# First modulation vectors: half of the columns by split products, half in full precision; first tiles transposed beside their copies

## The chip, the cores and the metric

The kernel runs on one core of one Trainium2 chip. The metric is the device time of one execution in microseconds (us); the time of a kernel is the median of several runs. The engines are named as in the profile: PE (matrix products), PEld (its weight loads), DVE (VectorE), ACT (ScalarE), POOL (GpSimd) and SP, which here only issues transfers. ACT issues some transfers too. Each engine works through its own instructions in the order in which they stand in the program.

## What is computed

One layer of a generative model: 2048 latent tokens and 256 context tokens of width 1024 pass a gated linear recurrence in both directions, then a gated feed-forward layer with a short convolution. What matters here is the very start. Two conditioning vectors, `c` for latent tokens and `c_ctx` for context tokens, give shift, scale and gate vectors by one product with `w_ada` (1024 by 6144):

```
sc_lat, sc_ctx = jax.nn.silu(c), jax.nn.silu(c_ctx)
m_l = (sc_lat @ w_ada[l] + b_ada[l])[:, None, :]
m_c = sc_ctx @ w_ada[l] + b_ada[l]
sh1, sc1, g1, sh2, sc2, g2 = jnp.split(m_l, 6, axis=-1)
hl = modulate(rmsnorm(lat, norm_g[l, 0]), sh1, sc1)
hc = modulate(rmsnorm(cx, norm_g[l, 0]), csh1, csc1)
yc, yl = hgrn2_mixer(hc, hl, ...)      # begins with h @ w_in, 1024 by 5120
```

Nothing of the recurrence can begin before the first 2048 columns of that product (shift and scale of the mixer) are there for both kinds of tokens. The other columns are worked out later, beside other work.

## The kernel before

All tokens are cut into 18 tiles of 128. Three tiles make a unit of 384 columns; six units follow each other for each of 8 heads. The first unit is context tile 0, context tile 1 and latent tile 0. A tile is normalized in place (ACT squares it and sums, DVE and POOL make the reciprocal root `rs`, DVE multiplies; helper `normalize`, L100 to L105, called by `early_x`), transposed by PE in two groups `g` of four 128-wide blocks (`transpose_mod`, L112), and multiplied and shifted by the modulation vectors A and B while it is copied out of PSUM: by ACT (L116) or by DVE (L119). The result `hm` is then split into a rounded part `hh` (ACT, L80) and a remainder `hl` (DVE, L81) by the helper `split`. All large products are sums of three products of such parts, rounded with rounded, rounded with remainder and remainder with rounded (`mm3`, L356 to L358); weights are split the same way into `wh` and `wl`, `vh` and `vl`, after their load into a tile `raw`.

The first stage (L189 to L232) works out the modulation vectors. `w_ada` comes in 16 transfers of 512 KB, `i` = 0 for the shift and `i` = 1 for the scale, for each of 8 row blocks `k`; `i` = 0 is issued by ACT, `i` = 1 by SP. The tiles `wada` have 13 buffers, which the weights of head 0 use after them. For each, PE makes two products of 512 columns in full fp32 precision with the two activated vectors `silv` as weights; each such product stands in the trace as two MATMUL records. They collect in four PSUM tiles `mps`. ACT copies these to `m2` (L216), PE turns them by 16 small transposes into `mt` (L220), and DVE makes B and A of them (L223 to L225). Then come the two groups of the first three tiles:

```
for g in range(2):
    for j, hm in enumerate(hms):
        transpose_mod(staged[j], hm, g, p0s, A1[m], B1[m], "tr", 3, (g + j) % 2)
        put_split(hm, 0, j, ks)
```

After that stands the normalization of four more tiles (`early_x(3)` to `early_x(6)`), whose transposes and splits are spread among the products of unit 0 of head 0: `unit` gets them as a list `todo`, and `tick`, called after each group of three products, takes the next one when it is due. In that first unit, `ticks = [0, 20]`: the six of them are due at even steps over 20 groups, the first one at once. From head to head the order is a pipeline: `load_feat` and `load_vg` load and split the weights of a head (five transfers of 512 KB for head 0).

A planner in the language's layer orders the instructions on each engine by its own estimate of their times, so the order in the program need not be that of the source. A transfer waits until the transfer eight places before it has landed; SP holds all transfers behind one that waits.

Of the kernel before, what the change touches and what calls it, by code (L numbers as in the profile page):

```python
# [23 lines left out]
KT = 8  # L24
# [24 lines left out]
def body(ctx, tc, a, out):  # L49
    nc = tc.nc  # L50
    pe, act, dve, pool, sp = nc.tensor, nc.scalar, nc.vector, nc.gpsimd, nc.sync
# [27 lines left out]
    def split(h, l, src):  # L79
        act.activation(h, src, AF.Copy)  # L80
        dve.tensor_tensor(l, src, h.bitcast(F32), OP.subtract)  # L81
# [22 lines left out]
        else:  # L104
            dve.tensor_scalar(xt, xt, rs, None, OP.mult)  # L105

    def transpose_mod(xt, hm, g, psp, A, B, tag, bufs, on_act):

        tp = psp.tile([128, 4, 128], F32, name="tp", tag=tag, bufs=bufs)
        for j in range(4):  # L110
            k = g * 4 + j
            pe.transpose(tp[:, j, :], xt[:, k * 128:(k + 1) * 128], ident)  # L112
        for j in range(4):
            k = g * 4 + j
            if on_act:
                act.activation(hm[:, k, :], tp[:, j, :], AF.Identity, bias=B[:, k:k + 1],  # L116
                               scale=A[:, k:k + 1])
            else:
                dve.tensor_scalar(hm[:, k, :], tp[:, j, :], A[:, k:k + 1], B[:, k:k + 1],  # L119
                                  OP.mult, OP.add)  # L120

    ch = ctx.enter_context(ExitStack())
    rawp = pool_(ch, "rawp", 2)
# [62 lines left out]
    with ExitStack() as c0:  # L186
# [2 lines left out]
        act.activation(sil, vec[:, V_C:V_C + 16], AF.Sigmoid)  # L189
        dve.tensor_tensor(sil, sil, vec[:, V_C:V_C + 16], OP.mult)  # L190
        silv = sil.rearrange("p (two k) -> p k two", two=2)
        mps = [p0s.tile([2, 512], F32, name=f"mps{n}") for n in range(4)]
# [10 lines left out]
        for k in range(KT):  # L203
            for i in range(2):
                wt = p0.tile([128, D], F32, name="wada", tag="wada", bufs=13)
                (sp if i else act).dma_start(
                    wt, a["w_ada"][k * 128:(k + 1) * 128, i * D:(i + 1) * D])
                for n in range(2):
                    pe.matmul(mps[2 * i + n], silv[:, k, :], wt[:, n * 512:(n + 1) * 512],
                              start=k == 0, stop=k == KT - 1)  # L210
            if 3 <= k < 6:
                early_x(k - 3)
        head0 = load_feat(0, p=p0, tag="wada", bufs=13)
        m2 = [rawp.tile([2, 2, 512], F32, name="m2", tag="raw") for _ in range(2)]
        for n in range(4):
            ada_done = act.activation(m2[n // 2][:, n % 2], mps[n], AF.Copy)  # L216
        m2f = [m.rearrange("p a b -> p (a b)") for m in m2]
        mt = p0s.tile([128, 16, 2], F32, name="mt")
        for j in range(16):
            pe.transpose(mt[:, j, :], m2f[j // 8][:, j % 8 * 128:(j % 8 + 1) * 128],  # L220
                         ident[0:2, 0:2])
        for i in (1, 0):
            dve.tensor_tensor(B1[i], mt[:, 0:8, i], vec[:, V_BA:V_BA + 8], OP.add)  # L223
            dve.tensor_tensor(A1[i], mt[:, 8:16, i], vec[:, V_BA + 8:V_BA + 16], OP.add)
# [54 lines left out]
    def mixer_scan():  # L279
# [82 lines left out]
        def unit(h, w, u, tiles, todo, fine=False):  # L362
# [1066 lines left out]
```

## Time and profile before

| | us |
|---|---|
| median of 3 runs | 2864.17 (2862.56 to 2865.4) |
| the profiled execution's own time | 2865.12 |
| its span, from first to last instruction | 2863.1 |
| PE busy in it | 2805.9 (98%) |
| DVE busy | 2110.5 (74%) |
| ACT busy | 1174.4 (41%) |
| first product of unit 0 starts | 41.52 |
| first product of unit 1 starts | 70.78 |

How to read it: PE is busy nearly all the time once the first unit has begun, so what the first 75 us lose or gain is found at the end again unless something later absorbs it. All places in time below are counted in us from the start of the span. A row of the timeline gives start, duration, engine, line, operation, output and inputs, how many instructions are merged in the row, and in brackets how long the engine had sat idle and for what. Durations of products overlap, so their rate is read from the distance of their starts.

### The profile page before, as it was taken

The page shows a single profiled execution, that of the slowest core. Times are in us where ns is not written, and L with a number is a line of the kernel's source. Part 1 is how long each engine was busy: PE and PEld are TensorE (multiplying, and loading weights), DVE is VectorE, ACT ScalarE, POOL GpSimd, SP SyncE. Part 2 cuts the span into 40 slices and gives each one's busy share as a digit, 9 for nine tenths or more (in the row PEclk, how much of TensorE's full clock was granted, in tenths as well). Part 3 has the DMA queues.
Part 4 walks back from the last instruction along what each step waited for, and adds up shares of the span by engine and source line. Part 5 has one row for each costly group of instructions (what it writes and reads, how often), then busy time and mean ns, then how long its engine had stood idle before and what let it go on. Part 6 is the DMA issues. An engine that isn't in the chain of part 4 may idle for free.

```text
span 2863.1 us, 43709 instructions
## 1 busy us (share of the span) xinstructions
PE 2805.9 (98%) x16016; PEld 2506.1 (88%) x16016; DVE 2110.5 (74%) x3690; ACT 1174.4 (41%) x2515; POOL 594.3 (21%) x1028
## 2 busy tenths in 40 slices
PE   7999999999999999998999799999999999999999
PEld 4999999999999999997888688888888888887887
DVE  5766666677666666577987698887888887677887
ACT  5433333365333333333555444444444444333343
POOL 2111111121111111111111353343444432000001
PEclk9999999999999999999999899999999999999999
DMA  6222222222222222135677622225522224887663
GB/s 236 69 80 77 84 79 78 78 86 81 85 90 71 84 69 87 62 94 183 266 290 276 257 88 89 82 81 176 206 88 71 77 89 136 284 298 251 196 203 122
DMA packets 202911, 386.56 MB, mean 135 GB/s; under 512 B 26692, under 2 KB 117828, under 8 KB 197448
## 3 DMA queue, kind: packets, MB, share of 16 engines
q1 hardware_dynamic: 199960, 375.51, 39.1%
q10 hardware_dynamic: 2736, 8.26, 0.8%
q8 instruction: 126, 2.06, 0.3%
q14 instruction: 89, 0.73, 0.1%
HBM read 281.70 MB, written 101.99 MB: 134 GB/s over the span
## 4 chain that ended last, share of the span: by engine, by line
PE 89%; DVE 4%; DMA 3%; ACT 2%; issue 1%; POOL 1%; SPq 0%; DVEq 0%; ACTq 0%; POOLq 0%
PE z L358 10%; PE z L356 10%; PE z L357 10%; PE y L1263 4%; PE y L1262 4%; PE y L1261 4%; PE zc L741 3%; PE zd L741 3%; PE zd L738 3%; PE zc L738 3%; PE zc L740 3%; PE zd L740 3%; PE za L741 3%; PE za L738 3%; PE za L740 3%; PE kv L574 2%
## 5 line engine op out<-in xcount | busy, mean ns | idle before, releaser
L356 PE MATMUL z<-vh,hh 128*128 128x256 f32 (+1 forms) x1024 | 300.3, 293 | 0.0
L358 PE MATMUL z<-vh,hl 128*128 128x256 f32 (+1 forms) x1024 | 293.5, 287 | 0.0
L357 PE MATMUL z<-vl,hh 128*128 128x256 f32 (+1 forms) x1024 | 293.3, 286 | 0.0
L356 PE MATMUL z<-hh,wh 128*128 128x384 f32 x768 | 264.0, 344 | 0.7 <-ACT hh L80 0.7
L357 PE MATMUL z<-hl,wh 128*128 128x384 f32 x768 | 258.5, 337 | 0.5 <-DVE hl L81 0.5
L358 PE MATMUL z<-hh,wl 128*128 128x384 f32 x768 | 258.7, 337 | 0.0
L1263 PE MATMUL y<-wd,ml 128*128 128x512 f32 x600 | 234.0, 390 | 2.3 <-DVE ml L81 2.1
L1261 PE MATMUL y<-wd,mh 128*128 128x512 f32 x600 | 233.8, 390 | 0.7 <-DVE P L1315 0.6
L1262 PE MATMUL y<-wd,mh 128*128 128x512 f32 x600 | 233.4, 389 | 0.0
L356 PEld LDWEIGHTS z<-vh,hh 128*128 128x128 f32 x1024 | 196.3, 192 | 0.0
L357 PEld LDWEIGHTS z<-vl,hh 128*128 128x128 f32 x1024 | 196.1, 191 | 0.0
L358 PEld LDWEIGHTS z<-vh,hl 128*128 128x128 f32 x1024 | 195.7, 191 | 0.0
L81 DVE TENSOR_TENSOR w<-s,w 128x512 fp32r<-128x512 f32 x132 | 145.1, 1106 | 61.6 <-ACT w L80 61.6
L484 POOL COPY TX<-S 128x3 f32<-128x3 f32 x48 | 14.6, 305 | 791.9 <-DVE S L448 791.9
L80 ACT ACTIVATE w<-raw 128x512 fp32r<-128x512 f32 x176 | 109.1, 628 | 111.6 <-DMA raw<-in_w_up_dram 43.9
L424 DVE TENSOR_TENSOR st<-z,st 128x128 f32<-128x128 f32 x127 | 36.6, 289 | 158.4 <-ACT st L423 158.2
L81 DVE TENSOR_TENSOR w<-raw,w 128x512 fp32r<-128x512 f32 x176 | 122.9, 701 | 40.4 <-ACT w L80 40.0
L1025 DVE SCALAR_TENSOR_TENSOR r<-uv,conv,r 128x1023 f32<-128x1023 f32 (+1 forms) x88 | 149.5, 1716 | 0.4
L356 PEld LDWEIGHTS z<-hh,wh 128*128 128x128 f32 x768 | 145.3, 189 | 4.4 <-DVE acc L620 1.7
L419 ACT ACTIVATE v<-z 128x128 f32<-128x128 f32 x128 | 35.5, 278 | 271.1 <-PE z L358 271.0
L357 PEld LDWEIGHTS z<-hl,wh 128*128 128x128 f32 x768 | 145.1, 189 | 0.7 <-DVE hl L81 0.7
L358 PEld LDWEIGHTS z<-hh,wl 128*128 128x128 f32 x768 | 144.8, 188 | 0.0
(325 smaller groups left out, 8172.9 us busy)
## 6 DMA issues: line engine op xcount, KB each, us to landing
raw<-in_w_up_dram SPq DMA_DIRECT2D x90, 512.0 KB, 3.9
raw<-in_w_in_dram SPq DMA_DIRECT2D x80, 512.0 KB, 3.7
lr<-m SPq DMA_DIRECT2D x49, 512.0 KB, 5.6
m<-r SPq DMA_DIRECT2D x66, 256.0 KB, 4.7
raw<-in_w_ada_dram SPq DMA_DIRECT2D x32, 512.0 KB, 4.4
stash<-st SPq DMA_DIRECT2D x125, 128.0 KB, 1.9
kq<-stash SPq DMA_DIRECT2D x15, 1024.0 KB, 7.3
og<-stash SPq DMA_DIRECT2D x15, 1024.0 KB, 6.4
```

The source lines that it names most:

```text
L80: act.activation(h, src, AF.Copy)
L81: dve.tensor_tensor(l, src, h.bitcast(F32), OP.subtract)
L356: pe.matmul(o, sh[:, k], mh[:, k], start=k == 0, stop=False)
L357: pe.matmul(o, sh[:, k], ml[:, k], start=False, stop=False)
L358: pe.matmul(o, sl[:, k], mh[:, k], start=False, stop=k == KT - 1)
L738: pe.matmul(o, w[:, 0, k], r[:, :, 0, k], start=start and k == 0, stop=False, skip_group_check=True)
L740: pe.matmul(o, w[:, 0, k], r[:, :, 1, k], start=False, stop=False, skip_group_check=True)
L741: pe.matmul(o, w[:, 1, k], r[:, :, 0, k], start=False, stop=k == 3, skip_group_check=True)
L1025: dve.scalar_tensor_tensor(r, x, cw, r, OP.mult, OP.add)
L1261: pe.matmul(z, lh, rh, start=start, stop=False, skip_group_check=True)
L1262: pe.matmul(z, lh, rl, start=False, stop=False, skip_group_check=True)
L1263: pe.matmul(z, ll, rh, start=False, stop=stop, skip_group_check=True)
```

## The change

For each transfer of `w_ada` the first 512 columns are still multiplied in full precision. The second 512 columns are split into a rounded part and a remainder (`w2`, a tile with two buffers; ACT for the one, DVE for the other) and multiplied in two products by `s4`, which holds the rounded parts and the remainders of the two vectors as four columns. So four of the eight full-precision records per row block become two products with split operands. The PSUM tile for them has four rows; after the small transposes DVE copies `mt` out of PSUM and adds the two remainder rows. `transpose_mod` is cut into `transpose4` and `modulate`, and the first group of transposes of the first three tiles stands before the small transposes. In the first unit `ticks` becomes `[-8, 20]`: the first transpose of the next tiles is due eight groups later.

```
+        s4 = p0.tile([128, KT, 4], F32R, name="s4")
+        split(s4[:, :, 0:2], s4[:, :, 2:4], silv)
+        mps = [p0s.tile([4 if n % 2 else 2, 512], F32, name=f"mps{n}") for n in range(4)]
+        tps = {}
...
+                w2 = rawp.tile([128, 2, 512], F32R, name="w2", tag="raw")
+                split(w2[:, 0], w2[:, 1], wt[:, 512:])
+                pe.matmul(mps[2 * i], silv[:, k, :], wt[:, 0:512],
+                          start=k == 0, stop=k == KT - 1)
                 for n in range(2):
-                    pe.matmul(mps[2 * i + n], silv[:, k, :], wt[:, n * 512:(n + 1) * 512],
-                              start=k == 0, stop=k == KT - 1)
+                    pe.matmul(mps[2 * i + 1], s4[:, k], w2[:, n],
+                              start=k == 0 and n == 0, stop=k == KT - 1 and n == 1)
...
+        m2 = [p0.tile([4, 512], F32, name=f"m2{n}") for n in range(4)]
         for n in range(4):
-            ada_done = act.activation(m2[n // 2][:, n % 2], mps[n], AF.Copy)
+            ada_done = act.activation(m2[n][0:2 + n % 2 * 2], mps[n], AF.Copy)
+        for j in range(3):
+            tps[0, j] = transpose4(staged[j], 0, p0s, "tr", 3)
...
+        mt = p0.tile([128, 16, 2], F32, name="mt")
+        dve.tensor_copy(mt, mt4[:, :, 0:2])
+        for j in (4, 12):
+            dve.tensor_tensor(mt[:, j:j + 4], mt[:, j:j + 4], mt4[:, j:j + 4, 2:4], OP.add)
...
-                transpose_mod(staged[j], hm, g, p0s, A1[m], B1[m], "tr", 3, (g + j) % 2)
+                if g:
+                    tps[g, j] = transpose4(staged[j], g, p0s, "tr", 3)
+                modulate(tps[g, j], hm, g, A1[m], B1[m], (g + j) % 2)
...
-            ticks = [0, 20 if s0 else 42]
+            late_ = fine == "late"
+            ticks = [-8, 20] if late_ else [0, 20 if s0 else 42]
...
-        steps, fine = 0, True
+        steps, fine = 0, "late"
```

The planner moves more than the diff shows. SP's transfers at the start, before (`vec` is small; `wada`, the tiles `x` and the weights `raw` are 512 KB each; `x_140` are the first three tiles, `x_141` and `x_142` the next four):

```order
L206 DMA wada<-in_w_ada_dram 128x1024 x2
L152 DMA x_140<-in_ctx_dram 128x1024
L206 DMA wada<-in_w_ada_dram 128x1024 x2
L152 DMA x_140<-in_ctx_dram 128x1024
L206 DMA wada<-in_w_ada_dram 128x1024 x2
L152 DMA x_140<-in_x_dram 128x1024
L206 DMA wada<-in_w_ada_dram 128x1024 x2
L162 DMA raw<-in_w_in_dram 128x1024 x5
L152 DMA x_141<-in_x_dram 128x1024 x3
L152 DMA x_142<-in_x_dram 128x1024
```

and now (`x_143` the first three tiles, `x_144` and `x_145` the next four):

```order
L218 DMA wada<-in_w_ada_dram 128x1024 x2
L160 DMA x_143<-in_ctx_dram 128x1024 x2
L218 DMA wada<-in_w_ada_dram 128x1024 x2
L160 DMA x_143<-in_x_dram 128x1024
L160 DMA x_144<-in_x_dram 128x1024
L218 DMA wada<-in_w_ada_dram 128x1024
L160 DMA x_144<-in_x_dram 128x1024
L218 DMA wada<-in_w_ada_dram 128x1024
L160 DMA x_144<-in_x_dram 128x1024
L218 DMA wada<-in_w_ada_dram 128x1024
L160 DMA x_145<-in_x_dram 128x1024
L218 DMA wada<-in_w_ada_dram 128x1024
```

The five loads of `raw` for head 0, and two for head 1, follow there. The four tiles that came after the weights now come ahead of the last `w_ada` transfer.

ACT from the first copy of the vectors to the first modulated tile, before:

```order
L80 ACTIVATE vh<-raw 128x8x128
L216 ACTIVATE m_249<-mps_136 2x512
L216 ACTIVATE m_249<-mps_137 2x512
L216 ACTIVATE m_250<-mps_138 2x512
L216 ACTIVATE m_250<-mps_139 2x512
L80 ACTIVATE vh<-raw 128x8x128
L116 ACTIVATE hm<-tp,B_1_108,A_1_106 128x128 x4
L80 ACTIVATE vh<-raw 128x8x128
L80 ACTIVATE hh_290<-hm 128x4x128 x3
```

and now:

```order
L80 ACTIVATE wh<-raw 128x1024
L232 ACTIVATE m_317<-mps_140 4x512
L80 ACTIVATE wh<-raw 128x1024
L232 ACTIVATE m_319<-mps_142 4x512
L80 ACTIVATE vh<-raw 128x8x128 x3
L124 ACTIVATE hm<-tp,B_1_108,A_1_106 128x128 x4
L80 ACTIVATE hh_373<-hm 128x4x128 x2
L124 ACTIVATE hm<-tp,B_1_108,A_1_106 128x128 x4
L80 ACTIVATE hh_373<-hm 128x4x128 x2
```

All five splits of head 0's weights now stand ahead of the first modulated tile, where before the fifth stood behind it, and the third rounded part of group 0 (`hh`) now stands behind a modulation of group 1.

PE in unit 0, from the first product to the second group of transposes of the next tiles, now (before, the first four such transposes stood after the first 12 products and the next ones 21 products later):

```order
L383 MATMUL z<-hh_373,wl 128x384 x2
L112 MATMUL tp<-ident,x_144 128x128 x4
L381 MATMUL z<-hh_373,wh 128x384
L382 MATMUL z<-hl_374,wh 128x384
L383 MATMUL z<-hh_373,wl 128x384
```

The transposes stand after 27 products, the 24 of the first output and three of the second. From within unit 1 on, all engines have the same order as before.

More of the change, by code (lines that the diff above doesn't have):

```diff
@@ L112, in transpose_mod, with modulate @@
             pe.transpose(tp[:, j, :], xt[:, k * 128:(k + 1) * 128], ident)
+        return tp
+    def transpose_mod(xt, hm, g, psp, A, B, tag, bufs, on_act):
+        modulate(transpose4(xt, g, psp, tag, bufs), hm, g, A, B, on_act)
+    def modulate(tp, hm, g, A, B, on_act):
         for j in range(4):
@@ L191, in body @@
         silv = sil.rearrange("p (two k) -> p k two", two=2)
-        mps = [p0s.tile([2, 512], F32, name=f"mps{n}") for n in range(4)]
+        s4 = p0.tile([128, KT, 4], F32R, name="s4")
+        split(s4[:, :, 0:2], s4[:, :, 2:4], silv)
+        mps = [p0s.tile([4 if n % 2 else 2, 512], F32, name=f"mps{n}") for n in range(4)]
+        tps = {}
         staged = [v[:, i] for p, n in ((2, 3), (5, 3), (4, 1))
@@ L213, in body @@
         head0 = load_feat(0, p=p0, tag="wada", bufs=13)
-        m2 = [rawp.tile([2, 2, 512], F32, name="m2", tag="raw") for _ in range(2)]
+        m2 = [p0.tile([4, 512], F32, name=f"m2{n}") for n in range(4)]
         for n in range(4):
-            ada_done = act.activation(m2[n // 2][:, n % 2], mps[n], AF.Copy)
-        m2f = [m.rearrange("p a b -> p (a b)") for m in m2]
-        mt = p0s.tile([128, 16, 2], F32, name="mt")
+            ada_done = act.activation(m2[n][0:2 + n % 2 * 2], mps[n], AF.Copy)
+        for j in range(3):
+            tps[0, j] = transpose4(staged[j], 0, p0s, "tr", 3)
+        mt4 = p0s.tile([128, 16, 4], F32, name="mt4")
         for j in range(16):
-            pe.transpose(mt[:, j, :], m2f[j // 8][:, j % 8 * 128:(j % 8 + 1) * 128],
-                         ident[0:2, 0:2])
+            n = j // 4
+            r = 2 + n % 2 * 2
+            pe.transpose(mt4[:, j, 0:r], m2[n][0:r, j % 4 * 128:(j % 4 + 1) * 128],
+                         ident[0:r, 0:r])
+        mt = p0.tile([128, 16, 2], F32, name="mt")
+        dve.tensor_copy(mt, mt4[:, :, 0:2])
+        for j in (4, 12):
+            dve.tensor_tensor(mt[:, j:j + 4], mt[:, j:j + 4], mt4[:, j:j + 4, 2:4], OP.add)
         for i in (1, 0):
```

2 lines of the change are left out of this document (1 added, 1 removed).

## The prediction

> **What bounds the kernel now.** The page first, the chain of work that ended last.
>
> ```profile
> PE 89%; DVE 4%; DMA 3%; ACT 2%; issue 1%; POOL 1%; SPq 0%; DVEq 0%; ACTq 0%; POOLq 0%
> ```
>
> PE carries 89% of the chain. What the change touches is the start, so next the windows of 10 us (from:to; length, then busy us and instructions of PE, PEld, DVE, ACT and POOL; granted clock; DMA share; GB/s) and PE's waits from 34 to 71 us.
>
> ```profile
> 20.00:30.00 10.00, 10.00 (x24) 1.96 (x23) 1.04 (x3) 1.76 (x3) 0.54 (x1) 1.00 1.03 410
> 30.00:40.00 10.00, 8.76 (x48) 4.12 (x46) 6.78 (x17) 8.18 (x14) 0.00 (x0) 1.00 1.02 408
> 40.00:50.00 10.00, 3.86 (x20) 2.94 (x19) 8.79 (x17) 9.81 (x21) 1.37 (x2) 0.87 0.39 156
> 50.00:60.00 10.00, 10.00 (x52) 9.80 (x51) 7.47 (x19) 4.77 (x13) 2.12 (x4) 0.79 0.01 2
> ...
> PE tp L112 <- DVE x L105: 4.9, 1, 4.9
> PE tp L112 <- ACT hm L116: 2.2, 2, 1.2
> ```
>
> Two things bound the start. Up to 40 us the transfers run at their limit, 410 GB/s, and PE is busy with the vectors until 35. From 37 to 50, ACT (9.81 of 10) and DVE (8.79) are full and PE waits for them; the largest wait, 4.9 us, is for the normalization of the fourth tile, because its transposes stand in PE's queue after 12 products. The timelines of PE and PEld give the rates:
>
> ```profile
> 20.24 0.09 PEld L209 LDWEIGHTS mps<-wada,sil 128*2 128x2 f32 x1 [0.34 <-issue]
> 20.67 0.09 PEld L209 LDWEIGHTS mps<-wada,sil 128*2 128x2 f32 x1 [0.34 <-issue]
> ...
> 4.89 30.11 PE L209 MATMUL mps<-wada,sil 128*2 128x512 f32 x64 [4.89 <-DVE sil L190]
> 42.41 0.44 PE L357 MATMUL z<-hl,wh 128*128 128x384 f32 x1 [0.45 <-DVE hl L81]
> 44.09 0.33 PE L357 MATMUL z<-hl,wh 128*128 128x384 f32 x1
> 44.26 0.34 PE L358 MATMUL z<-hh,wl 128*128 128x384 f32 x1
> 49.53 1.11 PE L112 MATMUL tp<-ident,x 128*128 128x128 f32 x4 [4.93 <-DVE x L105]
> 51.08 0.52 PE L358 MATMUL z<-hh,wl 128*128 128x384 f32 x1
> 51.40 0.52 PE L356 MATMUL z<-hh,wh 128*128 128x384 f32 x1
> 54.28 0.34 PE L356 MATMUL z<-hh,wh 128*128 128x384 f32 x1
> 70.78 0.42 PE L356 MATMUL z<-hh,wh 128*128 128x384 f32 x1
> ...
> 2600.03 0.40 PE L1261 MATMUL y<-wd,mh 128*128 128x512 f32 x1
> 2600.27 0.39 PE L1262 MATMUL y<-wd,mh 128*128 128x512 f32 x1
> ```
>
> A full-precision record of 512 columns costs 0.43 us, a split product of 512 columns 0.23, of 384 columns 0.17. After the 4.93 us wait the same product costs 0.32 until 54.28 (granted clock 0.79 in that window): the 12 products there lose 12 x 0.15 = 1.8 us. Last, a group of four transposes (a row of the chain of waits) and the work of ACT and DVE:
>
> ```profile
> 56.04 0.44 PE tp L112 x4
> ...
> 29.39 1.06 ACT L80 ACTIVATE wh<-raw 128x1024 fp32r<-128x1024 f32 x1 [3.59 <-DMA raw<-in_w_in_dram]
> 31.95 1.06 ACT L80 ACTIVATE vh<-raw 128x1024 fp32r<-128x1024 f32 x1 [0.23 <-DMA raw<-in_w_in_dram]
> 37.46 1.51 ACT L116 ACTIVATE hm<-tp,B,A 128x128 f32<-128x128 f32 x4 [0.89 <-DVE A L224]
> 39.80 1.67 ACT L80 ACTIVATE hh<-hm 128x512 fp32r<-128x512 f32 x3
> 48.08 1.06 ACT L100 ACTIVATE junk<-x 128x1024 f32<-128x1024 f32 x1 [0.19 <-ACT junk L100]
> 62.63 1.16 ACT L103 ACTIVATE xt<-xt,rs 128x1024 f32<-128x1024 f32 x1 [0.93 <-POOL rs L77]
> ...
> 33.04 1.23 DVE L81 TENSOR_TENSOR vl<-raw,vh 128x1024 fp32r<-128x1024 f32 x1
> 42.28 1.36 DVE L119 TENSOR_SCALAR hm<-tp,A,B 128x128 f32<-128x128 f32 x4
> 47.25 0.69 DVE L81 TENSOR_TENSOR hl<-hm,hh 128x512 fp32r<-128x512 f32 x1
> 51.09 0.75 DVE L105 TENSOR_SCALAR x<-x,rs 128x1024 f32<-128x1024 f32 x1 [0.73 <-POOL rs L77]
> 52.62 0.76 DVE L105 TENSOR_SCALAR x<-x,rs 128x1024 f32<-128x1024 f32 x1 [0.71 <-POOL rs L77]
> 55.08 0.48 DVE L404 TENSOR_SCALAR F<-F,oml,lb 128x384 f32<-128x384 f32 x1 [0.42 <-ACT F L402]
> ```
>
> The first three weight loads of head 0 land 1.28 us apart (the two rows of ACT that wait for them are the first and the third), which is 512 KB at the limit; the first is the 20th such transfer (16 of `w_ada`, three tiles). One normalization follows another on DVE after 1.53 us.
>
> **The change part by part.** *Products of the vectors.* 32 of the 64 records (0.43) become 32 split products (0.23): 6.4 us less PE work. No row of these lines has such an operand with four columns; 0.23 is the nearest row's, and a bound above is 0.43, no gain. But the saving needs the data sooner, and the transfers are full. Before, the last `w_ada` tile was the 19th transfer, at 29.39 - 1.28 = 28.1, ahead of PE's need. Now four more tiles go first: it is the 23rd, at 29.39 + 3 x 1.28 = 33.2. After it come its split on ACT (0.6, as `hh`), on DVE (0.69) and the last products: about 35, where PE ended before. The 6.4 us are spent on waiting for transfers.
>
> *New work on ACT and DVE.* 16 splits of 512 columns cost ACT 16 x 0.55 = 9 and DVE 16 x 0.69 = 11 us, under the transfers' cover (ACT is busy 1.8 and DVE 1.0 of 10 us from 20 to 30). Without that cover it would be the DVE's 11 us. The two buffers of `w2` tie the three engines together: one `w_ada` tile costs PE 2 x 0.43 + 2 x 0.23 = 1.32 us, less than the 33.2 / 16, about 2 us, at which they come. Nothing.
>
> *The start of modulation.* The five weight loads of head 0 are now transfers 24 to 28 and land at 34.5, 35.8, 37.1, 38.4 and 39.65. ACT takes all five before its first `hm`, so that begins no sooner than 39.65 + 1.06 = 40.7. DVE has, after the third of them (ACT ends it at 38.7), `vl` 1.15, the sums for A and B 0.5, the fourth `vl` 1.15, then A: 41.7. Before: 37.4. That is **+4.3 us**. The early transposes take 0.44 us a group off PE at a time when it is not waited for: nothing.
>
> *To the first products.* From 41.7: ACT modulates one tile (1.5, to 43.2), splits two (to 44.3), modulates group 1 of the first tile (from its transposes at 43.7; 1.5, to 45.8), splits it (46.3), and only then the third tile of group 0 (46.9); DVE ends `hl` at 47.7. The first products run from there, 42.41 before: **+5.3**. PE has idled since 38, so the 12 run at 0.32, as they did at 51.08: to 51.6. Meanwhile group 1 is ready: `hm` on ACT to 48.4, one square (1.06 and a short read of its sum), two `hh` to 50.6, `hl` to 51.3; no wait.
>
> *The later transposes.* 15 more products at 0.17 reach 54.2: 27 products and no transposes, where before 24 products and one group (0.44) were done at 54.28. The 4.93 us wait and most of the second slow stretch are gone, and they pay for the 5.3: **0 so far**, give or take.
>
> *What DVE still owes.* Before, four of the next tiles were normalized at 53.4. Now they begin after `hl` at 51.3 and end at 51.3 + 0.75 + 3 x 1.55 = 56.7, **3.4 us later**, since three weight splits (3 x 1.15) fell behind 35 us that lay ahead of it. Behind them stand `F` (0.5) and the first `hm` of the next unit (1.3): 58.5. That PSUM tile has one buffer, so PE's second group of transposes, due at 57.4, waits 1.1. DVE then catches up in unit 0, but the sixth group now falls into unit 1: first product there at 71.2 (70.78 before), after qz and ACT's two scalings of 1.1 each; transposes to 72.0, `hm` 73.6, `hh` 74.2, `hl` 74.9, where PE had 12 products and little else. Its 27th product of that unit ends at 76.9 instead of 75.8: **+1.1 us**, and from there the order is that of before.
>
> Sum: 2865.12 + 1.1 = 2866.2 for the profiled execution; that lies 0.95 over the median shown, so a median of 2864.17 + 1.1 = **2865.3**. The chain's steps are each good to half a microsecond or so, together 3.5: 2862 to 2869.
>
> **Rivals.** *Faster: the weights do not hold the modulation.* If the last `w_ada` tile and the five weight loads land four transfers earlier, at their old places in the stream, everything up to the first products moves by 4 x 1.28 = 5.1 us, and PE's idle time before the 12 slow products is short enough that they run at 0.17 (another 1.8): 1.1 - 5.1 - 1.8 = -5.8, 2858.4. For it: ACT's `w_ada` transfers have their own queue and may overtake. Against: 410 GB/s in every window to 40, and SP's queue keeps its order, in which the four tiles now stand first.
>
> *Slower: DVE never catches up.* The 3.4 us stay, because unit 1 gives DVE no idle time, and each group of transposes adds a wait as the 1.1 above: 3.4 + 2 x 1.1 = 5.6, 2869.8. It decides if DVE's first modulation of unit 1's last tile ends later than about 70. Against: in the window from 50 to 60 DVE is busy only 7.47 of 10.
>
> *Slower: the clock does not rise while PE waits for transfers.* At the start one record takes 0.85, twice 0.43:
>
> ```profile
> 8.26 0.13 PEld L209 LDWEIGHTS mps<-wada,sil 128*2 128x2 f32 x1 [0.72 <-issue]
> 9.11 0.13 PEld L209 LDWEIGHTS mps<-wada,sil 128*2 128x2 f32 x1 [0.72 <-issue]
> ```
>
> If it stays so, a `w_ada` tile costs 2.64 and 16 cost 42 us from 4.9 on: the vectors end 12 us later, 2877. Against: at 2.64 per tile PE would never wait, and unbroken work is what raised the rate here after 5 us. The Trainium skill ("TensorE: Matmul & The Clock Gate", section "Loop structure matters more than you think") warns that a long DMA wait between matmuls lets the clock fall to half, and its table ahead of that puts the limit near 3 us of idle time; the 4.93 us wait agrees with it, and by that rule the gaps forecast here, under 1 us, would not do it.
>
> **How the numbers follow.** What a measurement of this kernel can tell from no change is about 0.2%, 5.7 us. Chances: the forecast 0.56, the faster rival 0.16, DVE never catching up 0.2, the slow clock 0.08. The faster rival lies just beyond 5.7, so faster 0.16; of the DVE case some 0.15 goes beyond, with the clock slower 0.23; the same 0.61. The range reaches to 2858 on the one side and past the DVE case to 2872 on the other, and leaves out the slow clock.
>
> **What would show it.** Right: in the new profile the last `w_ada` lands near 33, DMA stays at 410 GB/s to 40, ACT's first `hm` follows its fifth weight split at 41 to 42, the first product of unit 0 stands at 47 to 48, no wait of 4.9 us, and unit 1 begins near 71. Wrong: a first `hm` at 37 or sooner (the faster rival), record distances of 0.85 past 15 us (the clock), or waits of PE on DVE's `hm` past 75 us (DVE).

## The result, and the profile after

| | before | after |
|---|---|---|
| median of 13 runs, us | 2863.84 (2862.14 to 2865.44) | 2870.29 (2865.04 to 2874.42) |
| the profiled execution's own time | 2865.12 | 2867.54 |
| its span | 2863.1 | 2865.8 |

The ratio of the medians is 1.0021, with a 95% interval of 1.0013 to 1.0029: a loss of 6.45 us, small, but its interval leaves out 1. The forecast was 2865.3, with 2858 to 2872 as its range. The time lies in the range, but 5 us above the forecast. The new profile's execution is one of the shorter of its kernel.

The chain of work that ended last, by engine, in the profile after:

```profile
PE 90%; DVE 4%; DMA 2%; ACT 2%; POOL 1%; issue 1%; DVEq 0%; POOLq 0%; ACTq 0%; SPq 0%
```

As before the change, PE carries the chain, so the start is again the place to look. Its windows after (from:to; length, busy us and instructions of PE, PEld, DVE, ACT and POOL; granted clock; DMA share; GB/s):

```profile
10.00:20.00 10.00, 6.24 (x15) 0.93 (x14) 5.50 (x14) 5.61 (x10) 6.31 (x25) 0.92 1.03 413
20.00:30.00 10.00, 9.55 (x25) 1.43 (x23) 3.84 (x7) 2.82 (x5) 0.54 (x1) 0.91 1.02 407
30.00:40.00 10.00, 8.69 (x41) 3.05 (x41) 4.60 (x6) 5.79 (x10) 0.00 (x0) 1.00 0.97 370
40.00:50.00 10.00, 3.60 (x18) 2.63 (x18) 9.38 (x25) 8.81 (x18) 0.00 (x0) 0.62 0.50 191
```

From 20 to 30 PE is nearly full although it has less to do than before, and part of that window runs at a lower granted clock (0.91). From 30 to 40 the transfers move 370 GB/s, where 410 had been forecast to 40. From 40 to 50 PE has 3.60 us of work: it waits for the modulation, as before, but later. PE's waits up to 90 us (engine, tile and line, what it waited for; us in total, times, longest), after:

```profile
PE mps L222 <- DMA wada<-in_w_ada_dram: 7.0, 4, 4.9
PE tp L112 <- ACT hm L124: 5.7, 2, 5.0
PE qz L461 <- DVE hm L127: 2.2, 1, 2.2
PE mps L225 <- DVE w L81: 1.9, 1, 1.9
PE mps L225 <- DVE rs L76: 1.5, 1, 1.5
```

The 4.9 us wait for a normalization (`x`) is gone; the 4.9 us for `wada` is the wait for the first tile, as long as the first wait before. New are waits inside the products of the vectors (`mps`): for DVE's `w`, and for late `w_ada` tiles. (Where a row names `rs`, DVE had ended the remainder `w` just before it, at 12.2.) PE's timeline after, at the places that the prediction named:

```profile
12.29 0.40 PE L225 MATMUL mps<-w,s 128*4 128x512 f32 x1 [1.53 <-DVE rs L76]
17.21 1.00 PE L225 MATMUL mps<-w,s 128*4 128x512 f32 x3 [1.93 <-DVE w L81]
18.14 3.28 PE L222 MATMUL mps<-wada,sil 128*2 128x512 f32 x4
34.40 1.02 PE L222 MATMUL mps<-wada,sil 128*2 128x512 f32 x2 [0.70 <-DMA wada<-in_w_ada_dram]
38.04 0.47 PE L225 MATMUL mps<-w,s 128*4 128x512 f32 x1
50.81 0.69 PE L382 MATMUL z<-hl,wh 128*128 128x384 f32 x1
57.80 0.60 PE L112 MATMUL tp<-ident,x 128*128 128x128 f32 x4
61.35 0.66 PE L112 MATMUL tp<-ident,x 128*128 128x128 f32 x4 [0.15 <-DVE hm L127]
73.67 0.30 PE L461 MATMUL qz<-ident,qt 128*128 128x128 f32 x1 [2.21 <-DVE hm L127]
74.87 0.42 PE L381 MATMUL z<-hh,wh 128*128 128x384 f32 x1
```

The last product of the vectors starts at 38.04 and, at its rate of 0.23 us, ends about 38.3. Before, the last record started at 34.40 and, at 0.43, ended about 34.8 (the row in the prediction reaches to 35.0, since its modelled end is longer). So the vectors end 3.5 us later. The first product of unit 1 stands at 74.87, against 70.78 before: 4.1 us. What made the vectors late stands in ACT's and DVE's timelines after. ACT first (`ACTq` rows are transfers that ACT issues):

```profile
23.52 0.63 ACT L80 ACTIVATE w<-wada 128x512 fp32r<-128x512 f32 x1 [3.60 <-PE mps L225]
23.76 0.33 ACTq L218 DMA_DIRECT2D wada<-in_w_ada_dram  x1
...
27.16 0.63 ACT L80 ACTIVATE w<-wada 128x512 fp32r<-128x512 f32 x1 [2.49 <-PE mps L225]
27.63 0.34 ACTq L218 DMA_DIRECT2D wada<-in_w_ada_dram  x1
...
40.55 2.93 ACT L80 ACTIVATE vh<-raw 128x1024 fp32r<-128x1024 f32 x3
44.55 1.50 ACT L124 ACTIVATE hm<-tp,B,A 128x128 f32<-128x128 f32 x4 [1.07 <-DVE A L248]
```

ACT's splits of `w_ada` wait for PE to free one of two buffers, and ACT's share of the transfers stands behind those splits. The last is issued at 27.63 and lands at 34.4, where PE waits for it. Before the change ACT issued its last two at 17.4:

```profile
17.39 0.82 ACTq L206 DMA_DIRECT2D wada<-in_w_ada_dram  x2
```

DVE and POOL, after:

```profile
4.46 5.46 POOL L273 TENSOR_TENSOR e<-eb,e 128x32 f32<-128x32 f32 x1 [2.89 <-DVE sil L198]
15.22 0.55 POOL L77 TENSOR_TENSOR rs<-rs,mhalf 128x1 f32<-128x1 f32 x1
...
15.80 0.75 DVE L105 TENSOR_SCALAR x<-x,rs 128x1024 f32<-128x1024 f32 x1 [3.50 <-POOL rs L77]
16.47 1.28 DVE L81 TENSOR_TENSOR w<-wada,w 128x512 fp32r<-128x512 f32 x2
...
43.16 1.22 DVE L81 TENSOR_TENSOR vl<-raw,vh 128x1024 fp32r<-128x1024 f32 x1
44.29 0.24 DVE L248 SCALAR_TENSOR_TENSOR A<-A,vec 128x8 f32<-128x8 f32 x2
```

DVE waits 3.50 us for POOL's first root, which comes behind a power of 5.46 us and some masks and memsets; a remainder of `w_ada` is queued behind that wait. That is PE's 1.93 us wait at 17.21, and after it four records take 3.2 us instead of 1.7 (half rate).

How much of the 4.1 us reaches the end? When the start of the same product is compared in the two traces, the kernel after is 4.3 us later at 221 us, 4.8 later at 2553, but only 2.5 later at 2598. There, in the last stage, which the change does not touch, PE waits for DVE's `ml` in one execution and not in the other (at 2598.3 for 1.97 us before, not at all from 2540 to 2600 after). Rows of PE's waits from 2540 us to the end, before:

```profile
PE y L1263 <- DVE ml L81: 2.1, 2, 2.0
```

and after:

```profile
PE y L1290 <- DVE ml L81: 0.7, 1, 0.7
```

### The profile page after: what moved, and what is told of

Read it like the earlier page. It is cut to its first block, busy times and chain, and to the rows that moved or that the text cites. A ratio compares the mean times of both kernels' runs of the same rounds, so it can differ in the third digit from the quotient of the medians.

```text
span 2865.8 us, 43769 instructions
## 1 busy us (share of the span) xinstructions
PE 2804.3 (98%) x16016; PEld 2506.2 (87%) x16016; DVE 2121.3 (74%) x3710; ACT 1181.6 (41%) x2532; POOL 588.3 (21%) x1028
## 4 chain that ended last, share of the span: by engine, by line
PE 90%; DVE 4%; DMA 2%; ACT 2%; POOL 1%; issue 1%; DVEq 0%; POOLq 0%; ACTq 0%; SPq 0%
PE z L383 10%; PE z L381 10%; PE z L382 10%; PE y L1290 4%; PE y L1288 4%; PE y L1289 4%; PE zd L768 3%; PE zc L768 3%; PE zc L765 3%; PE zd L765 3%; PE zc L767 3%; PE zd L767 3%; PE za L768 3%; PE za L765 3%; PE za L767 3%; PE kv L601 2%
```

## The experiments

Times of 5 to 11 runs each, interleaved with the kernel before on the same chip. There were four sets of runs, and the kernel before had its own median in each: 2865.88 (the changed kernel again, four buffers, SP issuing, full-precision products kept), 2866.2 (later tiles held, GpSimd issuing, both runs on the ticks), 2865.93 (GpSimd's long work, all split, the last three weight splits) and 2864.49 (the last of these once more). So ratios are compared, and medians only within a set. "Unit 1" is the start of its first product (70.78 before, 74.87 after); "vectors" the end of the last product of the modulation vectors, reckoned from its start as above (34.8 before, 38.3 after).

**The changed kernel again**, unchanged.

> The changed kernel once more, unchanged, for a second profile. In its first profile the products of the vectors end at 38.3 (34.8 before), unit 1 begins at 74.87 (70.78 before), the offset to the kernel before is +4.0 to +4.9 us from 80 to 2552 us and +2.5 at the end; its run times spread over 9 us. Theory 'ring' (the two buffers of w2 tie ACT's splits, and the transfers that ACT issues behind them, to PE): vectors end at 38 to 39 again and unit 1 begins near 75, since all of that is order and no chance; ratio 1.001 to 1.003. Theory 'clock' (the spread comes from where in the first 60 us the granted clock falls): vectors or unit 1 move by 2 us or more from the first profile, with the granted clock's windows from 10 to 30 us moving along.

Measured: 2872.68 (ratio 1.0025, 1.0014 to 1.0036). Vectors 38.5, unit 1 at 75.06, last `w_ada` issued by ACT at 27.74: the start repeats to 0.2 us, as "ring" said. But the offset to the kernel before is +5.7 at 221 us instead of +4.3. The difference is in the granted clock just after the start of unit 1. Windows of 3.4 us in the second profile:

```profile
72.50:75.90 3.40, 1.33 (x10) 1.15 (x10) 2.87 (x11) 1.46 (x4) 0.00 (x0) 1.00 0.00 0
75.90:79.30 3.40, 3.40 (x13) 3.30 (x12) 1.57 (x5) 2.13 (x5) 0.00 (x0) 0.51 0.09 24
79.30:82.70 3.40, 3.40 (x22) 3.36 (x21) 0.00 (x0) 0.47 (x2) 0.00 (x0) 0.99 0.00 0
```

and the middle one of the same windows in the first profile:

```profile
75.90:79.30 3.40, 3.40 (x21) 2.96 (x20) 1.38 (x4) 2.40 (x6) 0.00 (x0) 1.00 0.07 19
```

After the same two waits (2.2 and 0.7 us) 13 instructions fit into these 3.4 us in one execution, 21 in the other. So the start's own loss repeats with the order, and some 1.4 us on top of it came in one execution and not in the other.

**Four buffers for the split parts.**

```
-                w2 = rawp.tile([128, 2, 512], F32R, name="w2", tag="raw")
+                w2 = (p0.tile([128, 2, 512], F32R, name="w2", tag="w2", bufs=2) if i else
+                      rawp.tile([128, 2, 512], F32R, name="w2", tag="raw"))
```

> The changed kernel with four buffers for w2 in place of two (two for each half of w_ada). Theory 'ring': ACT no longer waits for PE's products before its next split, so its last w_ada transfer is issued by 22 (27.6 with two buffers) and lands by 33 (34.4); the products end at 35 to 36.5 instead of 38.3, unit 1 begins 1.5 to 3 us sooner than 74.87, and the median is 2 to 3 us below that of two buffers. Rival 'order' (what holds the vectors is that the transfers of four more tiles stand ahead, whatever the buffers): last landing and end of the products move by less than 0.7, the median stays within 1 us of that of two buffers. Rival 'clock': the products end later or earlier with the length of the stretch of granted clock 0.5 near 18 to 22 us, not with the transfer.

Measured: 2874.01 (1.003, 1.0018 to 1.0041); vectors 40.7, unit 1 at 79.33. A miss: the theory expected a gain. The planner now puts 11 splits ahead of ACT's last transfer (10 with two buffers), and all but one of ACT's waits there are for a tile instead of a buffer, so that transfer is issued at 30.28 and PE waits 11.0 us for `w_ada` (7.0 with two buffers). The number of buffers alone is not what holds the stream; ACT's queue, in which transfers stand behind splits, is a candidate.

**All `w_ada` transfers issued by SP.**

```
-                (sp if i else act).dma_start(
+                sp.dma_start(
```

> The changed kernel with all w_ada tiles issued by SP, none by ACT; SP then has the four later tiles between and behind them. Theory 'ring': no transfer stands behind a split of ACT, so the transfers run without a gap at 410 GB/s, the last w_ada lands at 30 to 32, products end at 34.5 to 36.5, the five weight loads land by 40 as before, ACT's first hm at 41 to 42.5 (44.55 in the changed kernel), median 2 to 3.5 us below the changed kernel. Rival 'order': the weight loads behind the same 23 transfers set the first hm, whoever issues w_ada: first hm within 0.7 of 44.55 and the median within 1 us of the changed kernel's.

Measured: 2865.21 (0.9997, 0.9988 to 1.0006): 7.5 us below the changed kernel in the same set of runs, and not to be told from the kernel before. ACT's first `hm` starts at 38.38. PE's timeline of this kernel:

```profile
14.18 1.02 PE L222 MATMUL mps<-wada,sil 128*2 128x512 f32 x2
15.13 0.63 PE L225 MATMUL mps<-w,s 128*4 128x512 f32 x2
15.69 1.02 PE L222 MATMUL mps<-wada,sil 128*2 128x512 f32 x2
...
34.23 0.39 PE L225 MATMUL mps<-w,s 128*4 128x512 f32 x1
44.98 0.69 PE L382 MATMUL z<-hl,wh 128*128 128x384 f32 x1
70.98 0.67 PE L381 MATMUL z<-hh,wh 128*128 128x384 f32 x1
```

Without the hold the products run unbroken from 10 to 30 and end at 34.5; first products 5.8 and unit 1 3.9 us sooner than in the changed kernel. And the rows show what the split is worth at best (a row block has two tiles, so four split products stand in place of four records, not two as the description of the change says): one tile costs 0.95 for the two full records and 0.56 for the two split products, 1.51 in all, against 4 x 0.43 = 1.72 before. That is 0.21 x 16 = 3.4 us, and the early transposes, which now stand among these products, take part of it back. Two other things changed with the issuer, though. The planner put the last `w_ada` and head 0's five weights ahead of the four later tiles again. And the first tile is normalized only at 19.84, so DVE's wait for GpSimd's first root is 0.67 us instead of 3.50. The next three runs were to separate these.

**The four later tiles held behind the weight loads**, ACT still issuing its half.

```
-        for j in range(3, 7):
-            early_x(j)
+        with tc.issue_after(loaded[0].ins):
+            for j in range(3, 7):
+                early_x(j)
```

(`loaded[0]` is the third weight load of head 0.)

> The changed kernel with the transfers of the four later tiles held behind the last weight load of the third type of head 0, so that SP has them behind the five weight loads, as before the change; ACT still issues its half of w_ada between its splits. In the changed kernel the last w_ada is issued by ACT at 27.6 and lands at 34.4, products end at 38.3, first hm at 44.55. Theory 'held' (ACT's transfers stand behind ACT's splits, those behind PE): the last w_ada is still issued at 27 or later and the products end at 36.5 to 38.5; only the weight loads land sooner (the fifth by 36 to 37), so the gain is 2 us at most. Theory 'order' (the four tiles ahead are what costs): last w_ada lands by 30, products end by 35.5, first hm by 41, the median 4 to 7 us below the changed kernel (2870 to 2873 in the runs so far).

Measured: 2869.45 (1.0016, 1.0007 to 1.0026). The last `w_ada` is issued at 28.15, vectors 37.1, first `hm` 42.77, unit 1 at 73.86. "Held" said 36.5 to 38.5 for the vectors and a gain of 2 us at most in the time; "order" wanted 35.5 and a first `hm` by 41. SP has the five weights ahead of the four later tiles here, as before the change, and DVE's 3.50 us wait for GpSimd is still there. The order alone is worth about 1 us at unit 1.

**ACT's half issued by GpSimd.**

```
-                (sp if i else act).dma_start(
+                (sp if i else pool).dma_start(
```

> The changed kernel with ACT's half of the w_ada transfers issued by GpSimd instead, which has no splits; SP's order stays with the four later tiles ahead of the last w_ada. Theory 'held': the last w_ada lands by 31 to 33.5 in place of 34.4, the products end at 35 to 36.5 in place of 38.3, first hm at 41 to 43, median 2 to 4 us below the changed kernel. Theory 'order': products end within 0.7 of 38.3, since the same 23 transfers stand ahead, and the median is within 1.5 us of the changed kernel's. In the two sent last, SP issuing everything took back all of the loss; together with the fifth run this one tells which half of that it was.

Measured: 2877.51 (1.0044, 1.0032 to 1.0057); vectors 44.8, unit 1 at 81.15. This told nothing apart: GpSimd's first transfer lands at 8.3 instead of 4.8, and its last two are issued at 23.85 and later, behind a root for which GpSimd itself had waited 9.53 us. It replaced one held queue by another. So how much of SP's gain is the free issue by itself is not measured.

**GpSimd's long work put behind the roots.** SP's order and the splits are those of the changed kernel; only the first power of 5.5 us, the masks and the memsets, all needed later, are moved behind the first three roots.

```
-        pool.tensor_tensor(e2f, eb, e2f, OP.pow)
+        with tc.issue_after(rs_done.ins):
+            pool.tensor_tensor(e2f, eb, e2f, OP.pow)
```

> The changed kernel with GpSimd's first power of 5.5 us, masks and memsets (all needed later) put behind the reciprocal roots of the first three tiles; all else, SP's order of transfers too, as in the changed kernel. There DVE waits 3.5 us at 12.3 for GpSimd's first root, the remainder of a w_ada tile stands behind that wait, PE waits 1.5 and 1.9 us for it, and after that its records run at half rate for 3.3 us. Theory 'root' (that wait starts the delay): DVE's wait falls below 1 us, PE's two waits and the slow stretch go, the last w_ada is issued by 24 (27.6) and lands by 31.5 (34.4), products end by 36 (38.3), first hm by 42.5 (44.55), the median 1.5 to 3 us below the changed kernel's. Theory 'held' alone (ring of two and ACT's queue, whatever DVE waits for at 12): last w_ada issued within 1 us of 27.6, products end within 0.7 of 38.3, median within 1.5 us.

Measured: 2870.26 (1.0017, 1.0008 to 1.0026). That lies within the intervals of both results of the changed kernel (1.0013 to 1.0029, 1.0014 to 1.0036), so the time does not show a gain; the trace does. Rows of its timelines, DVE, ACT and PE:

```profile
11.98 0.75 DVE L107 TENSOR_SCALAR x<-x,rs 128x1024 f32<-128x1024 f32 x1 [0.75 <-POOL rs L79]
...
25.84 0.33 ACTq L220 DMA_DIRECT2D wada<-in_w_ada_dram  x1
...
36.23 0.47 PE L227 MATMUL mps<-w,s 128*4 128x512 f32 x1
73.06 0.42 PE L387 MATMUL z<-hh,wh 128*128 128x384 f32 x1
```

DVE's 3.50 us wait is 0.75, PE's slow records at 18 are gone, the last transfer is issued 1.8 us sooner, the vectors end at 36.5, and unit 1 begins 1.8 us sooner. "Root" had the direction; its bounds (issued by 24, vectors by 36) were half a microsecond to two too early. GpSimd's moved work stops DVE once more, at 25 and 27, and PE waits 1.2 us for a remainder at 28.6. So the wait for GpSimd's root, with all that hangs on it, is 1.8 us of the vectors' delay of 3.5. By themselves the order (1.0) and the root (1.8) make 2.8 of the 3.9 us that SP's run took back at unit 1; the other 1.1 would be the free issue if the three simply added up, which no run shows.

**Full-precision products kept**, with the early transposes, the separate copies and the ticks of the change.

```
-                for n in range(2):
-                    pe.matmul(mps[2 * i + 1], s4[:, k], w2[:, n],
-                              start=k == 0 and n == 0, stop=k == KT - 1 and n == 1)
+                pe.matmul(mps[2 * i + 1], silv[:, k, :], wt[:, 512:1024],
+                          start=k == 0, stop=k == KT - 1)
```

> The changed kernel with all products of the vectors in full precision (64 records of 0.43 us, no splits, no w2); early transposes, copies and ticks [-8,20] stay. Theory 'ring': without splits nothing holds ACT's transfers, so the last w_ada lands near 33 and the 64 records end near 35 to 36.5, sooner than the 38.3 that the 32 + 32 take; first hm at 41 to 42.5, unit 1 near 71 to 72.5, median 2 to 4 us below the changed kernel, that is 2864 to 2867. Rival 'split pays' (the split products do save their 6.4 us and what costs is the order of the transfers or the ticks): products end at 41 or later and the median is that of the changed kernel or above.

Measured: 2867.5 (1.0007, 0.9998 to 1.0016), vectors 35.1, first `hm` 39.84, unit 1 at 70.56, offset 0.0 us at 221. With no splits nothing holds ACT (its last two transfers go out at 17.2), and the planner puts SP's transfers back into the order of before (the last `w_ada` lands at 27.9, where the forecast had 33). The products end where they ended before. So the loss of the start belongs to the split products together with what they tie up and the order that the planner makes of it. The first `hm` still comes 2.4 and the first products 3.7 us later than before, but unit 1 does not: the early transposes and the ticks cost nothing there.

**The ticks undone in the changed kernel.**

```
-            ticks = [-8, 20] if late_ else [0, 20 if s0 else 42]
+            ticks = [0, 20 if s0 else 42]
```

> The changed kernel with the first transposes of the next tiles due at once again (ticks [0,20]). The prediction's step: the later ticks remove a wait of some 5 us for a normalization and the slow products behind it. By that, a wait of 2 to 5 us on DVE's x returns at 53 to 55 and the median is 2 to 6 us above the changed kernel's 2870 to 2873. Rival: the wait only moves to a later group or into unit 1 (PE's wait for qz of 2.2 us at 73.7), and the median is within 1.5 us of the changed kernel's.

Measured: 2872.56 (1.0026, 1.0016 to 1.0037), the changed kernel's time. PE's timeline:

```profile
18.44 1.88 PE L222 MATMUL mps<-wada,sil 128*2 128x512 f32 x4
...
37.79 0.47 PE L225 MATMUL mps<-w,s 128*4 128x512 f32 x1
...
55.59 0.60 PE L112 MATMUL tp<-ident,x 128*128 128x128 f32 x4
...
73.35 0.66 PE L112 MATMUL tp<-ident,x 128*128 128x128 f32 x4 [2.12 <-DVE hm L127]
...
76.22 0.67 PE L381 MATMUL z<-hh,wh 128*128 128x384 f32 x1
```

The transposes stand at 55.59, and no wait for `x` comes back: the first products are 8 us later than before, so the normalizations are done by then. The wait appears in another form, for `hm`, at 73.35, and unit 1 begins 1.2 to 1.4 us later than with the new ticks. That is in the trace, not in the medians.

Up to 44 us ACT, DVE, GpSimd and SP have the same order here as in the changed kernel, so this is a third execution of its start. The clock stayed full this time: four records at 18.44 take 1.8 us. The vectors end at 38.0 all the same (38.3 and 38.5 with the slow stretch). So the clock is not what made the vectors late.

**The ticks alone, in the kernel before.** The same line, put into the old kernel.

> The kernel before with ticks [-8,20] alone: no split products, no early transposes. By the prediction's step the 4.9 us wait at 49.5 goes, and the 1.8 us of slow products behind it; unit 1 begins 2 to 6 us sooner than 70.78 and the median is 2 to 5 us below that of before: a version faster than both. Rival: DVE's order behind it makes PE wait in unit 1 for the sixth group, as in the run without splits (same unit 1 as before, although its first products were 4 us later), and the median is within 1.5 us of before.

Measured: 2867.87 (1.0011, 1.0002 to 1.0019): no gain. Rows of PE's waits to 90 us, and its first product of unit 1:

```profile
PE tp L112 <- ACT hm L116: 3.3, 2, 2.1
PE z L356 <- ACT hh L80: 3.2, 3, 2.3
PE tp L112 <- DVE hm L119: 2.7, 1, 2.7
...
70.57 0.62 PE L356 MATMUL z<-hh,wh 128*128 128x384 f32 x2 [0.16 <-ACT hh L80]
```

The 4.9 us wait is gone and unit 1 begins at 70.57 instead of 70.78. Even these 0.2 us are not the ticks' own: in this execution PE's records came to full rate at 8.1 us instead of 9.9, and the vectors ended 1.0 us sooner than in the profile before. The rival was right: the time turns into waits for `hh` and `hm`, while ACT is busy 9.58 and DVE 8.53 of 10 us from 40 to 50. In this execution PE also waits longer in the untouched last stage:

```profile
PE y L1264 <- DVE ml L81: 5.4, 6, 2.5
```

(2.1 us before the change, 0.7 after). Between 2553 us and the end this execution loses 4 us on the one before the change.

**All four products as split products**, SP issuing, four buffers.

```
+                for q in range(2):
+                    split(w2[:, 0], w2[:, 1], wt[:, q * 512:(q + 1) * 512])
+                    for n in range(2):
+                        pe.matmul(mps[2 * i + q], s4[:, k], w2[:, n],
+                                  start=k == 0 and n == 0, stop=k == KT - 1 and n == 1)
```

> SP issues all of w_ada, and all four products of 512 columns of each tile row are split products (four buffers for w2), none in full precision. In the run where SP issued everything a tile pair cost PE 1.51 us (two full-precision records 0.86, two split products 0.46, and 0.19 more where the kinds alternate), so PE was busy 10 of 10 us from 10 to 30 and the products ended at 34.6 although the last transfer landed at 28.8. Theory 'PE sets the end there': with 4 x 0.23 = 0.92 per tile the products end at 29.5 to 32, first hm at 34 to 37, unit 1 begins 2 to 4 us sooner and the median is 1 to 4 us below that run's 2865. Rival 'ACT and DVE set it': 32 splits cost ACT 32 x 0.55 and DVE 32 x 0.6 = 19 us plus the roots and normalizations, they fall behind the transfers, products end at 34 or later, and the median is that run's or above.

Measured: 2866.12 (1.0, 0.9992 to 1.0009). Vectors 32.3, first `hm` 37.38, unit 1 at 68.94. Each theory has a part: the products end 2.1 us sooner, not 2.6 to 5, while ACT (9.29) and DVE (9.30 of 10 us from 10 to 20) are nearly full and PE (8.23) is not; unit 1 gains 2.0 us on the run with SP; the time shows nothing.

**The last three weight splits behind the first modulated tile**, SP issuing.

```
+        with tc.issue_after(mods[0].ins), tc.issue_after(mods[1].ins):
+            load_w(0, 0, head0[1][:, :, 256:], head0[2][:, :, 256:], p=p0, tag="wada", bufs=13)
             load_vg(0, head0, p=p0, tag="wada", bufs=13)
```

(`mods` holds the last modulations of group 0 on DVE and on ACT.)

> SP issues all of w_ada, and the last three of head 0's five weight splits stand behind the first modulated tile on DVE and ACT, as most did in the kernel before. Where SP issued everything, the small transposes ended at 36.1 but the first modulated tile began at 38.4, with one weight remainder of 1.22 us on DVE in between and another behind it. Theory 'splits ahead of the vectors': first hm at 36.8 to 37.8, first products at 42 to 43.5 in place of 45, unit 1 at 69.5 to 71 in place of 70.98, median 0.5 to 2.5 us below that run's 2865. Rival 'DVE's total is what counts' (DVE is busy 9.4 of 10 us from 40 to 50 in any order, so what is put back is paid in a later wait): first products sooner, but unit 1 within 0.7 us and the median within 1.5 us.

Measured: 2864.39 (0.9994, 0.9985 to 1.0003); first `hm` 37.12, first products 42.07, unit 1 at 68.47. The splits were in the way: unit 1 comes 2.5 us sooner than with SP alone (ratio there 0.9997, so the time shows no difference). Once more:

> The kernel of the run before (SP issues all of w_ada, the last three weight splits behind the first modulated tile) once more, to see whether it beats the kernel before the change. Its first profile: unit 1 at 68.47 (70.78 before), offset to before -1.0 to -1.5 us from 87 to 2550 us and -4.8 at the end; ratio 0.9994 (0.9985 to 1.0003). If the gain of the start is real, unit 1 begins within 0.5 of 68.5 and the ratio lies at 0.999 to 0.9997; if the first result was chance, the ratio is 1.0000 or above. Either way the offset between 220 and 2550 us stays at -1 to -2: what lies beyond that at the end comes from the last stage, not from the start.

Measured: 2865.7 (0.9999, 0.999 to 1.0008); unit 1 at 69.13, offset to the kernel before -1.0 us at 221 and +1.0 at the end. The start is better than before the change by 1.7 to 2.3 us at unit 1 and by about 1 us later on; that is less than the time can show. Going by the ratios this version beats the changed kernel by 0.2 to 0.3%; that it beats the kernel before is not shown.

## Why the prediction was right in sign and small by 5 us

Its places against the first profile after (the first products by the first that reads `hl`, as in the forecast, at 42.41 before; the very first starts at 50.00):

| step | forecast | measured |
|---|---|---|
| last `w_ada` lands | 33.2 | 34.4 |
| products of the vectors end | 35 | 38.3 |
| first `hm` | 41.7 | 44.55 |
| first products of unit 0 | 47.7 | 50.81 |
| first transposes of the next tiles | 54.2 | 57.80 |
| wait at the second ones | 1.1 | 0.15 |
| unit 1 | 71.2 | 74.87 |

*Products of the vectors: the step that failed.* "About 35, where PE ended before" was 38.3, and every later place carries this: from the vectors' end to the first `hm` 6.7 was forecast and 6.25 measured, from there to the first products 6.0 and 6.26, to the transposes 6.5 and 7.0, and from the first `hm` to unit 1 29.5 and 30.3. Two assumptions stand behind the 35. One is that the transfers come without a gap, so that the 23rd lands at 33.2; it was issued too late for that. The other is 1.32 us of PE per tile, so that PE keeps up; it costs 1.51, and when the last tile came PE still had two tiles' full records and seven split products to do. The prediction's 0.23 for such an operand was right; what it lacked is the 0.19 that two kinds of product in turn cost.

*New work on ACT and DVE, "Nothing": wrong.* The sentence compared rates (1.32 under 2 us) and left out what is queued on the engines. DVE's remainder stood behind a normalization that waits for GpSimd (1.8 us, shown by moving GpSimd's work), and ACT's transfers stood behind splits that wait for PE. The second is shown only together with SP's order and without the wait for GpSimd: issuing all by SP takes back 3.8 us at the vectors and 3.9 at unit 1, the order alone 1.2 and 1.0, the root alone 1.8 and 1.8.

*The start of modulation.* The weights landed about as forecast (the first at 34.4, the fourth at 38.2), but ACT's three `vh` ran without a wait from 40.55: the weights did not hold them. The vectors held the modulation, with two remainders of weights ahead of A on DVE. That those remainders cost was right: with SP issuing, putting them back gained 1.8 to 2.5 us at unit 1.

*To the first products.* Right, mechanism and size; 15 products instead of 12 ran at 0.32.

*The later transposes, "0 so far".* The 4.93 us wait was counted as a gain of the ticks. It would have gone by itself, because the first products came later; and it was no loss of its own, since its removal alone in the kernel before brought no more than 0.2 us at unit 1. The ticks are worth 1.2 to 1.4 us there. The sum came out near since some 5 us were set on both sides of it, and that is luck.

*What DVE still owes.* The 1.1 us wait at the second transposes was 0.15; PE waited 2.2 us for DVE's `hm` ahead of qz instead. The rest of this step held: the sixth group fell into unit 1 (transposes at 75.31), and from unit 1's first product to its 28th the offset grew from 4.1 to 4.75 us, 0.65 where 0.7 had been forecast. So the forecast loss of 1.1 us has its sign from DVE's debt, while most of the measured loss comes from the vectors, which the forecast put at nothing; that the sign came out right is in part luck.

*The rivals.* The faster one would need the last `w_ada` four transfers earlier; with SP issuing it comes at 28.8, and even so the time is only that of before. "DVE never catches up" names a time, 2869.8, next to the one measured, but not its cause. Its sign did come (DVE's first modulation of unit 1's last tile ended at 73.5, not by 70), but DVE was late because the vectors were: without splits it ended at 69.2, against 67.9 before the change, and there the start lost nothing. The slow clock at 2877 did not come, though waits of 1.5 and 1.9 us were followed by one stretch of half rate, which cost 1.5 on the spot and at most 0.5 at the vectors' end. The Trainium skill ("TensorE: Matmul & The Clock Gate", section "Why this matters for your kernels") allows idle gaps up to about 3 us; by that rule the gaps of 2.2 and 0.7 us at 73 would be safe, and in the second profile they were not. The same page (section "What's actually happening") says that the activity window of 3413 ns is free-running, which agrees with the two profiles that differ after the same gaps.

*From the trace to the time.* 4.1 us at unit 1 are +4.3 and +5.7 at 221 us in the two profiles; the medians lie 6.45 and 6.8 above those of before. Part of the rest may be the clock at unit 1. In 7 of the 14 profiles, the changed kernel's second among them, a stretch of 3.4 or 6.8 us at half the granted clock stands between 69 and 87 us (in SP's run from 69.3 to 76.1 at 0.50), and there the offset to before grows by 1.8 to 3.1 us from unit 1's first product to its 28th. In the other variants it grows by 0.7 to 1.3; in the kernel before, one profile, no such stretch stands. How often it comes in the executions behind the medians no run shows, so the rest of 1 to 2 us stays open. The executions differ by some microseconds in the last stage (PE's waits for `ml` were 0.7 to 5.4 us in the profiles quoted), with the same order of instructions, and single profiles do not give its mean.

## What to carry to other kernels

A rate that fits on paper does not hide new work: look at what each engine's queue puts ahead of it and behind it, above all transfers issued by an engine that now waits, and short steps of one engine that wait for another's long ones. Where a stream of loads matters, try to issue it from an engine that has nothing to wait for: here that took the loss back, though the order of the transfers and a wait for GpSimd changed with it. A wait in a profile is not a gain to be had: the largest wait at the start could be taken out alone, and unit 1 began no more than 0.2 us sooner, while ACT and DVE were nearly full. And a single profile has its own share of slow clock: compare the same stretch in several executions before giving it a cause.

## What the runs showed of the hardware

The granted clock fell to half (0.51 over 3.4 us) after gaps of 2.2 and 0.7 us in one execution and stayed at 1.00 in another of the same kernel. Two kinds of product in turn cost more than each by itself: in the run with SP issuing, two split products stand 0.23 us apart and two full-precision records 0.43, but a tile of both takes 1.51 us where 1.32 add up; the two changes of kind cost 0.19. A power of 128x32 elements kept GpSimd 5.46 us, and one of 128x1 0.55.
